# A two-layer decoder trunk on one core: the input turned once, low parts and gate outputs placed differently in layer one, and unread products ahead of the first loads

## The chip, the cores and the metric

The kernel runs on one core of one Trainium2 chip. Its time is the device time of the whole program in microseconds; the number given for a kernel is the median of several runs. TensorE (PE in the profile) multiplies matrices, with a separate queue for loading weights (PEld); VectorE (DVE), ScalarE (ACT) and GpSimd (POOL) do the element work; SyncE (SP) issues nearly all transfers between DRAM and the on-chip memory (SBUF). Products land in PSUM.

## The reference, cut to what matters

Sequence and model width are 1024, one batch, everything in f32. A vector `c` gives shifts, scales and gates for each layer (`ada = silu(c) @ ada_w + ada_b`). Layer one is:

```
h = rmsnorm(x, g0) * (1 + sc1) + sh1
q, k, v, ig, fg, og = split(h @ a_w_in)        # 512, 512, 1024, 8, 8, 1024 columns
hh = mlstm(q, k, v, ig, fg)                    # 8 heads, chunks of 128 tokens, running maximum
y  = (rmsnorm(hh) * sigmoid(og)) @ a_w_out
x  = x + g1 * rmsnorm(y, g1n)
x  = x + g2 * rmsnorm(sqrelu_mlp(rmsnorm(x) * (1 + sc2) + sh2), g3n)
```

Here `rmsnorm(x, g) = x * rsqrt(mean(x*x) + 1e-6) * g`. Layer two (latent attention on shared keys and values, and a second MLP) follows; the change doesn't touch its code.

## The kernel before, in words

**Numbers.** Every large product is made with f32 accuracy out of three matmuls (`mm3`, L235 to L238): each factor is split into a high part, rounded to the fast f32 format (fp32r), and a low part, the difference; the products low x high, high x low and high x high are added in PSUM. Weights come in pieces of 128 x 1024 (`wload`, L209 to L228): SP loads a piece into a tile `raw` (L216), ScalarE casts it to the high part (L193), and the low part is subtracted (L195) by VectorE and GpSimd in turn, by a counter. A variable `low[0]` puts all of them on one engine while it is set; before the change it is set only for the first weights (L1684).

**Layout.** The tokens are handled in two halves of 512, `hfs[0]` and `hfs[1]`. Activations are kept feature-major: eight tiles of 128 features x 512 tokens. The input comes token-major, so it has to be turned by TensorE, four transposes of 128 x 128 for one such tile.

**Buffers.** PSUM is divided among three rotating pools: `ps` (two tiles of 128 x 512), `pc` (two) and `pm` (two double tiles). Four `raw` tiles are shared by the weight pieces and by the pieces of `ada_w` (below).

**Who decides the order.** The program is written as generators that are woven together by hand (`drain`, `weave`, `in_turn`, `with_bg`); a scheduler then orders the instructions of each engine by its own simulated time line. `tc.high_priority` moves an instruction forward and `tc.issue_after` keeps it behind a given one. The order is fixed at build time; on the chip each engine runs its list in order and waits on semaphores.

**Background work.** `ada_chunk` (L353 to L372) computes 512 columns of `ada` on VectorE: four loads of 512 KB, and eight instructions (L363, L365) that multiply 128 rows each by one value of `c` and add, then a few small matmuls (L338 when alone, or four transposes). A version with matmuls (`ada_chunk_pe`, L326) does the shift at the start. `bgs` is a chain of sixteen such chunks, pulled one step at a time by `with_bg` beside other stages.

**The stages around the change**, in program order:

- `vector_columns`, then `first_norm` for half 0: `scale_rows` squares and sums each row on ScalarE (L496), gets 1/rms with some small instructions, multiplies the rows on VectorE (L503), and `turn` transposes them (L524); ScalarE copies the result to SBUF (L1655).
- `ada_first(0)`: the first 512 columns of scale and shift; L1644 makes the factor `A0`.
- The first three weight pieces; `modulate0` for the first four feature tiles (scale and shift on VectorE, L1662; high part on ScalarE, L1663; low part L1665), then `ada_first(1)`.
- `qk_pairs`: queries and keys of half 0, with the other four tiles of `modulate0` in between.
- `gates_in(hfs[0])`, woven with background chunks; it contains `gates0` (L681 to L730), a serial chain of small instructions on 8 x 512 elements, most of them on VectorE.
- `load_x1`; `v_in(hfs[0])` (values) woven with background chunks and `intra0` (the scores within a chunk).
- `scale_x1` (sums of squares and multiplication of the rows of half 1, L505 to L520), and `norm0`: transposes (L530) into `ps`, scale and shift on ScalarE (L532), high part on ScalarE or VectorE (L534), low part on VectorE or GpSimd (L538). `in_turn` weaves it with `og0(hfs[0])` (output gates) and `chunks0(hfs[0])` (the recurrence over chunks).
- For half 1: `gates_in`, `qk_in`, `split_o(hfs[0])` (L784, L786), `v_in` and `intra0`.
- `wout` of half 0 with `chunks0(hfs[1])`; `og0(hfs[1])` woven with `post(hfs[0])`; `wout(hfs[1])` woven with the rest of `post`; then `post(hfs[1])` with the MLP. `post` normalises the output, adds the input (`residual`, L941), and makes the MLP's input (`normed`, L479). The input that it adds comes from `x_rows` (L890): it loads the rows again and turns them again, eight tiles of four transposes (L901) into `pc`.

Of the kernel before, what the change touches and what calls it, by code (L numbers as in the profile page):

```python
# [9 lines left out]
F32 = mybir.dt.float32  # L10
# [4 lines left out]
ALU = mybir.AluOpType  # L15
# [67 lines left out]
def kernel(  # L83
# [69 lines left out]
    def pm():  # L153
        return pp.tile([P, 2, 512], F32, tag="pm", bufs=2, name=f"pm_{next(uid)}")

# [336 lines left out]
    def scale_rows(xt):  # L492
        st = small(4)
        for t in range(4):
            junk = pm()
            nc.scalar.activation(  # L496
                junk.rearrange("p a b -> p (a b)"), xt[t], AF.Square, accum_out=st[:, t : t + 1]
            )
        v, y, w = small(4), small(4), small(4)
        nc.vector.tensor_scalar(v, st, 1.0 / D, EPS, ALU.mult, ALU.add)  # L500
        rsqrt_(y, v, w)
        for t in range(4):
            nc.vector.tensor_scalar(xt[t], xt[t], y[:, t : t + 1], None, ALU.mult)  # L503

    def scale_x1(x1):  # L505
# [7 lines left out]
        v, y, w = small(4), small(4), small(4)  # L513
        nc.vector.tensor_add(v, st[:, 0:4], st[:, 4:8])
        nc.vector.tensor_scalar(v, v, 1.0 / D, EPS, ALU.mult, ALU.add)
        rsqrt_(y, v, w)
# [9 lines left out]
    def norm0(h, xt, A, sh):  # L526
        for k in range(KD):
            pt = ps()
            for t in range(4):
                nc.tensor.transpose(pt[:, ts(t, P)], xt[k // 4][t][:, ts(k % 4, P)], ident)  # L530
            u = tmc()
            nc.scalar.activation(u, pt, AF.Identity, bias=sh[:, k : k + 1], scale=A[:, k : k + 1])  # L532
            if k % 2:
                nc.vector.tensor_copy(h.hi[k], u)  # L534
            else:
                nc.scalar.copy(h.hi[k], u)
            e = nc.vector if k % 2 else nc.gpsimd
            e.tensor_sub(h.lo[k], u, h.hi[k].bitcast(F32))  # L538
# [340 lines left out]
    def wout(w, o, store, wide=False):  # L879

        for m in range(KD):
            pt = proj_fm(w, m * P, o, (lambda: pm()[:, 0]) if wide and m % 2 else ps)
# [6 lines left out]

    def x_rows(half):  # L890

        xt = []
        for t in range(4):
            a = hd() if half else k4()[:, :1024]
            nc.sync.dma_start(a, x_of[half * 4 + t])
            xt.append(a)

        def blk(k):
            pt = pc()
            for t in range(4):  # L900
                nc.tensor.transpose(pt[:, ts(t, P)], xt[t][:, ts(k, P)], ident)  # L901
            return pt

        return blk
# [743 lines left out]
    def first_norm():  # L1648

        scale_rows(x0)  # L1650
# [5 lines left out]
        return xT  # L1656

    def modulate0(h, xT, j):
        A, sh = A0, adac(0, SH1)
        for k in range(4 * j, 4 * j + 4):  # L1660
            u = tmc()
            nc.vector.tensor_scalar(u, xT[k], A[:, k : k + 1], sh[:, k : k + 1], ALU.mult, ALU.add)  # L1662
# [14 lines left out]

    vector_columns()
    xT0 = first_norm()
    drain(ada_first(0, k4))  # L1680

# [27 lines left out]
    def in_turn(wide, steps, fill):  # L1709
# [271 lines left out]
```

## Time and profile before

| what | value |
|---|---|
| median of 3 runs | 2415.41 us (2413.01 to 2417.33) |
| profiled execution, its own time | 2414.08 us |
| its span from first to last instruction | 2412.3 us |
| granted TensorE clock, mean | 0.998 |
| read from and written to DRAM | 313.24 MB and 55.05 MB |
| instructions in the span | 30656 |

The profile is of one execution. It gives the busy time of each engine, divides the span into slices, follows the work that ended last back to the start (the chain of waits), and lists groups of instructions as: line, engine, operation, tile written <- tiles read, shape, count, then busy time and mean length (ns), then the idle time of the engine just before them and what ended it. The timeline lists instructions in order of time as: start, length, engine, line, operation, with the idle time before in brackets. The view of stretches gives busy time per engine in a stretch, then the granted clock (1.00 is full), the share of the 16 DMA engines, and GB/s.

### The profile page before, as it was taken

Reading aid. Unit: us, or ns where it says so; the run is one execution under the profiler, and the core shown is the slowest. Engines: PE = TensorE matmul, PEld = TensorE weight load, DVE = VectorE, ACT = ScalarE, POOL = GpSimd, SP = SyncE. Lnnn points to the kernel's source line nnn. Section 1 sums busy time; section 2 is a strip of 40 time slices with the busy share of each in tenths; the row PEclk is TensorE's granted clock in tenths of the full one; section 3 lists DMA queues with packets and bytes.
Section 4 is the critical chain, followed back from the end, with each engine's and each line's share of the span. In section 5 each row is a group of like instructions: output and inputs, shape, how many; then the busy total and the mean of one; then the engine's idle time right before and its main releaser. Section 6 shows DMA issues by size and latency. Waiting matters only on the chain.

```text
span 2412.3 us, 30656 instructions
## 1 busy us (share of the span) xinstructions
PE 2369.8 (98%) x11669; PEld 1950.5 (81%) x11669; DVE 1476.4 (61%) x2269; ACT 1049.5 (44%) x1706; POOL 435.5 (18%) x269
## 2 busy tenths in 40 slices
PE   7999999999999999999999999999999999999998
PEld 5887787788888887888888877888888888888886
DVE  6576766958665667866664967554555385253335
ACT  4355334645333354434444554434444443443333
POOL 2131221300000000233421100332221102121121
PEclk9999999999999999999999999999999999999999
DMA  7442564444654745555543454774424454354431
GB/s 267 147 130 63 176 191 131 150 133 141 197 175 130 246 133 182 155 168 176 185 131 110 145 161 153 243 250 139 157 97 135 119 162 122 109 188 134 143 103 62
DMA packets 373843, 370.30 MB, mean 154 GB/s; under 512 B 24163, under 2 KB 282272, under 8 KB 373696
## 3 DMA queue, kind: packets, MB, share of 16 engines
q1 hardware_dynamic: 373408, 368.24, 48.6%
q8 instruction: 92, 1.51, 0.3%
q14 instruction: 55, 0.45, 0.1%
q0 software_dynamic: 288, 0.10, 0.0%
HBM read 313.24 MB, written 55.05 MB: 153 GB/s over the span
## 4 chain that ended last, share of the span: by engine, by line
PE 88%; DVE 6%; DMA 3%; ACT 2%; issue 1%; POOL 0%; SPq 0%; DVEq 0%; ACTq 0%
PE ps L236 16%; PE ps L237 16%; PE ps L238 16%; PE pm L236 9%; PE pm L238 9%; PE pm L237 9%; DMA raw<-in_mlp_w_dram 2%; PE pc L1456 1%; PE pc L236 1%; PE pm L811 1%; PE pc L238 1%; PE pc L237 1%; PE pm L1342 1%; PE pm L1336 1%; PE pm L1338 1%
## 5 line engine op out<-in xcount | busy, mean ns | idle before, releaser
L193 ACT CAST wh<-raw 128x1024 fp32r<-128x1024 f32 (+2 forms) x366 | 375.8, 1032 | 740.2 <-PE ps L236 356.3
L195 POOL TENSOR_TENSOR wl<-raw,wh 128x1024 fp32r<-128x1024 f32 (+2 forms) x158 | 379.8, 2409 | 1522.3 <-ACT wh L193 1356.7
L236 PE MATMUL ps<-k,wl 128*128 128x512 f32 x1528 | 611.4, 400 | 6.5 <-DVE wl L195 3.3
L237 PE MATMUL ps<-k,wh 128*128 128x512 f32 x1528 | 601.5, 394 | 0.0
L238 PE MATMUL ps<-k,wh 128*128 128x512 f32 x1528 | 600.8, 393 | 0.0
L195 DVE TENSOR_TENSOR wl<-raw,wh 128x1024 fp32r<-128x1024 f32 (+1 forms) x208 | 270.0, 1301 | 285.1 <-ACT wh L193 278.1
L236 PEld LDWEIGHTS ps<-k,wl 128*128 128x128 f32 x1528 | 287.0, 188 | 74.3 <-DVE wl L195 5.0
L238 PEld LDWEIGHTS ps<-k,wh 128*128 128x128 f32 x1528 | 287.0, 188 | 67.5 <-issue 0.5
L237 PEld LDWEIGHTS ps<-k,wh 128*128 128x128 f32 x1528 | 287.4, 188 | 63.0 <-issue 1.9
L203 DVE TENSOR_TENSOR k<-k,pm 128x512 f32<-128x512 f32 (+1 forms) x254 | 210.7, 859 | 130.3 <-PE pm L238 129.5
L476 DVE TENSOR_TENSOR hd<-tmp,hd 128x512 fp32r<-128x512 f32 x128 | 120.9, 945 | 205.5 <-ACT hd L475 205.2
L236 PE MATMUL pm<-hd,wl 128*128 128x512 f32 x512 | 201.8, 394 | 0.5 <-ACT hd L475 0.5
L237 PE MATMUL pm<-hd,wh 128*128 128x512 f32 x512 | 199.7, 390 | 0.7 <-DVE hd L476 0.7
L238 PE MATMUL pm<-hd,wh 128*128 128x512 f32 x512 | 200.0, 391 | 0.0
L236 PE MATMUL pm<-wh,hd 128*128 128x512 f32 x488 | 192.4, 394 | 2.8 <-ACT raw L1348 2.5
L237 PE MATMUL pm<-wl,hd 128*128 128x512 f32 x488 | 191.3, 392 | 0.0
L238 PE MATMUL pm<-wh,hd 128*128 128x512 f32 x488 | 191.1, 392 | 0.0
L365 DVE SCALAR_TENSOR_TENSOR tma<-raw,cond,tma 128x512 f32<-128x512 f32 x168 | 130.4, 776 | 20.9 <-DMA raw<-in_ada_w_dram 12.1
L1348 ACT ACTIVATE raw<-pm,sm 128x128 f32<-128x128 f32 (+3 forms) x64 | 47.4, 741 | 157.0 <-DVE sm L1347 126.7
L237 PEld LDWEIGHTS pm<-hd,wh 128*128 128x128 f32 x512 | 96.2, 188 | 21.6 <-DVE hd L476 1.0
L236 PEld LDWEIGHTS pm<-hd,wl 128*128 128x128 f32 x512 | 96.1, 188 | 21.4 <-ACT hd L475 0.9
L238 PEld LDWEIGHTS pm<-hd,wh 128*128 128x128 f32 x512 | 96.1, 188 | 21.0
(359 smaller groups left out, 3603.2 us busy)
## 6 DMA issues: line engine op xcount, KB each, us to landing
raw<-in_mlp_w_dram SPq DMA_DIRECT2D x256, 512.0 KB, 4.3
raw<-in_ada_w_dram SPq DMA_DIRECT2D x80, 512.0 KB, 4.4
raw<-in_a_w_in_dram SPq DMA_DIRECT2D x48, 512.0 KB, 4.6
xs<-k SPq DMA_DIRECT2D x40, 256.0 KB, 4.6
raw<-in_kv_ada_w_dram SPq DMA_DIRECT2D x16, 512.0 KB, 4.0
raw<-in_a_w_out_dram SPq DMA_DIRECT2D x16, 512.0 KB, 4.7
kd<-k SPq DMA_DIRECT2D x32, 256.0 KB, 3.5
vd<-k SPq DMA_DIRECT2D x32, 256.0 KB, 5.0
```

What stands on the lines that cost most here:

```text
L193: nc.scalar.copy(hi[:, :n], r[:, :n])
L195: i = e.tensor_sub(lo[:, :n], r[:, :n], hi[:, :n].bitcast(F32))
L203: return f(*a, **k)
L236: nc.tensor.matmul(o, ll, rh, start=start, stop=False)
L237: nc.tensor.matmul(o, lh, rl, start=False, stop=False)
L238: pe_last[0] = nc.tensor.matmul(o, lh, rh, start=False, stop=stop)
L365: nc.vector.scalar_tensor_tensor(acc, r[:, kk], cond[:, k : k + 1], acc, ALU.mult, ALU.add)
L476: nc.vector.tensor_sub(lo, u, hi.bitcast(F32))
L811: nc.tensor.matmul(nv[:, r, i], hf.PT[p_][:, r, cs], v[:, 2 * p_ + r], start=g == 0, stop=True,)
L1336: nc.tensor.matmul(o[:, :w], ql, kh, start=True, stop=False)
L1338: nc.tensor.matmul(o[:, :w], qT, kk[1][:, ks], start=False, stop=False)
L1348: nc.scalar.activation(pr[:, :n], f, AF.Exp, bias=m, scale=SCALE, accum_out=l)
```

## The change

Five parts:

1. **The input is turned once.** `first_norm` and `norm0` turn the raw input instead of rows that were multiplied by 1/rms. The turned tiles are stored to DRAM (`xt_d`): half 0 by four transfers of 512 KB after `qk_pairs`, half 1 by eight of 256 KB within `norm0`. `post` of the first layer loads them from there (`x_ahead(..., True)`), and `x_rows` with its transposes is gone.
2. **1/rms is applied after turning.** `along_tokens` spreads the four columns of 1/rms over a 128 x 512 tile with four matmuls against the identity and a copy by ScalarE. `modulate0` and `norm0` then use one scalar_tensor_tensor on VectorE (input x factor x 1/rms) and the existing `split_mod`: the high part with the shift on ScalarE (L478), the low part by another scalar_tensor_tensor on VectorE (L479). The multiplications of rows and GpSimd's part in them go.
3. **Unread products.** 24 bf16 matmuls of the identity with itself (128 x 512, in a `pc` tile that nothing reads) stand ahead of `vector_columns`, and five more behind the last TensorE instruction of `ada_first(0)`.
4. **Low parts and background.** `low[0]` is VectorE during `v_in`/`intra0` of half 0, and from `gates_in` of half 1 to the end of its `v_in`/`intra0`. `gates_in(hfs[0])` is no longer woven with background chunks. In `in_turn` the filling generator (`norm0`) takes a step every round instead of two of three.
5. **Alternating gates.** In `og0` of half 1 every other product uses a `pm` tile instead of `ps`, as `wout` did already.

```diff
+    def one_pm():
+        return pm()[:, 0]
...
-    def scale_rows(xt):
+    def along_tokens(dst, y):
+        pt = pc()
+        for t in range(4):
+            nc.tensor.matmul(
+                pt[:, ts(t, P)], y[:, t : t + 1].to_broadcast([P, P]), ident, start=True, stop=True
+            )
+        nc.scalar.copy(dst, pt)
+        return dst
+
+    def rms_rows(v):
+        nc.vector.tensor_scalar(v, v, 1.0 / D, EPS, ALU.mult, ALU.add)
+        y, w = small(4), small(4)
+        rsqrt_(y, v, w)
+        return y
+
+    def rms_x0(xt):
...
-        for t in range(4):
-            nc.vector.tensor_scalar(xt[t], xt[t], y[:, t : t + 1], None, ALU.mult)
-
-    def scale_x1(x1):
+        return rms_rows(st)
+
+    def rms_x1(x1):
...
-        for g in range(2):
-            for t in range(4):
-                e = nc.gpsimd if t % 2 else nc.vector
-                e.tensor_scalar(x1[g][t], x1[g][t], y[:, t : t + 1], None, ALU.mult)
+        return rms_rows(v)
...
-    def norm0(h, xt, A, sh):
+    xt_d = [scratch([D, H], f"xt{i}") for i in range(2)]
+
+    def norm0(h, xt, y, A, sh):
+        rstd = along_tokens(tmp(), y)
         for k in range(KD):
             pt = ps()
-            for t in range(4):
-                nc.tensor.transpose(pt[:, ts(t, P)], xt[k // 4][t][:, ts(k % 4, P)], ident)
-            u = tmc()
-            nc.scalar.activation(u, pt, AF.Identity, bias=sh[:, k : k + 1], scale=A[:, k : k + 1])
-            if k % 2:
-                nc.vector.tensor_copy(h.hi[k], u)
-            else:
-                nc.scalar.copy(h.hi[k], u)
-            e = nc.vector if k % 2 else nc.gpsimd
-            e.tensor_sub(h.lo[k], u, h.hi[k].bitcast(F32))
+            turn(xt[k // 4], pt, k % 4)
+            a, u = tmp(), tmc()
+            nc.scalar.copy(a, pt)
+            nc.sync.dma_start(xt_d[1][ts(k, P)], a)
+            nc.vector.scalar_tensor_tensor(u, pt, A[:, k : k + 1], rstd, ALU.mult, ALU.mult)
+            split_mod(h.hi[k], h.lo[k], u, sh[:, k : k + 1])
             yield
...
-            pt = proj_fm(w_in, 2064 + k * P, hf.h)
+            pt = proj_fm(w_in, 2064 + k * P, hf.h, one_pm if hf.i and k % 2 else ps)
...
-    def x_rows(half):
...
-    def x_ahead(alloc):
+    def x_ahead(alloc, first=False):
         def src(half):
             t = [alloc() for _ in range(4)]
+            of = xt_d[half] if first else xs[:, ts(half, H)]
             for b in range(4):
                 nc.sync.dma_start(
-                    t[b], xs[2 * b * P : (2 * b + 2) * P, ts(half, H)].rearrange("(k p) n -> p k n", p=P)
+                    t[b], of[2 * b * P : (2 * b + 2) * P].rearrange("(k p) n -> p k n", p=P)
                 )
...
     def first_norm():
-        scale_rows(x0)
+        y = rms_x0(x0)
...
-        return xT
+        return xT, along_tokens(Cst.rearrange("p a b -> p (a b)")[:, :H], y)
 
     def modulate0(h, xT, j):
...
-            nc.vector.tensor_scalar(u, xT[k], A[:, k : k + 1], sh[:, k : k + 1], ALU.mult, ALU.add)
-            nc.scalar.copy(h.hi[k], u)
-            e = nc.gpsimd if j and k % 2 else nc.vector
-            e.tensor_sub(h.lo[k], u, h.hi[k].bitcast(F32))
+            nc.vector.scalar_tensor_tensor(u, xT[k], A[:, k : k + 1], rs0, ALU.mult, ALU.mult)
+            split_mod(h.hi[k], h.lo[k], u, sh[:, k : k + 1])
...
+    def busy(n):
+        pt = pc()
+        for _ in range(n):
+            i = nc.tensor.matmul(
+                pt, identb, identb.unsqueeze(1).to_broadcast([P, 4, P]), start=True, stop=True
+            )
+        return i.ins.engine
+
+    pe_engine = busy(24)
     vector_columns()
-    xT0 = first_norm()
+    xT0, rs0 = first_norm()
     drain(ada_first(0, k4))
+    with tc.issue_after(last_on_pe()):
+        busy(5)
...
             if n % 3 < 2:
                 go(wide)
-                next(fill, None)
+            next(fill, None)
...
     drain(qk_pairs(hfs[0], w0, modulate0(hfs[0].h, xT0, 1)))
-    drain(with_bg(gates_in(hfs[0]), bgs, 1))
+    for b in range(4):
+        nc.sync.dma_start(
+            xt_d[0][2 * b * P : (2 * b + 2) * P].rearrange("(k p) n -> p k n", p=P), xT0.t[b]
+        )
+    drain(gates_in(hfs[0]))
     x1 = load_x1()
+    low[0] = nc.vector
     drain(weave(with_bg(v_in(hfs[0]), bgs, 1), intra0(hfs[0]), 1.5))
-    scale_x1(x1)
+    low[0] = None
+    y1 = rms_x1(x1)
     hfs[1].h = Split()
-    n1 = norm0(hfs[1].h, x1, A0, adac(0, SH1))
+    n1 = norm0(hfs[1].h, x1, y1, A0, adac(0, SH1))
     in_turn(og0(hfs[0], hdv), chunks0(hfs[0]), n1)
     drain(n1)
 
+    low[0] = nc.vector
     drain(gates_in(hfs[1]))
...
     drain(weave_n(with_bg(main, bgs, 1.7), intra0(hfs[1]), 0.8))
+    low[0] = None
...
-    p0 = post(hfs[0], y0, B0, x_rows, A1, adac(0, SH2))
+    p0 = post(hfs[0], y0, B0, x_ahead(k4v, True), A1, adac(0, SH2))
...
-    p1 = post(hfs[1], y1, B0, x_rows, A1, adac(0, SH2))
+    p1 = post(hfs[1], y1, B0, x_ahead(hdv, True), A1, adac(0, SH2))
```

More of the change, by code (lines that the diff above doesn't have):

```diff
@@ L512, in scale_x1 @@
                 )
[L513 removed]
+        v = small(4)
         nc.vector.tensor_add(v, st[:, 0:4], st[:, 4:8])
[L515 to L520 removed]
+        return rms_rows(v)
     def turn(xt, pt, k):
@@ L881, in wout @@
         for m in range(KD):
-            pt = proj_fm(w, m * P, o, (lambda: pm()[:, 0]) if wide and m % 2 else ps)
+            pt = proj_fm(w, m * P, o, one_pm if wide and m % 2 else ps)
             store(m, pt)
@@ L888 @@
     xs_blk = lambda k, half: xs[ts(k, P), ts(half, H)]
-    def x_rows(half):
[L892 to L904, printed above, removed]
     def x_cols(half):
@@ L1676, in w_parts, with last_on_pe @@
         return [t.rearrange("p (a b) -> p a b", b=256) for t in wsplit(r, D)]
+    def last_on_pe():
+        traced = nc.cur_bb.bb.instructions
+        return next(i for i in reversed(traced) if i.engine == pe_engine)
+    def busy(n):
[6 more added lines that the diff above has]
+    pe_engine = busy(24)
     vector_columns()
-    xT0 = first_norm()
+    xT0, rs0 = first_norm()
     drain(ada_first(0, k4))
+    with tc.issue_after(last_on_pe()):
+        busy(5)
     w0 = [w_raw(b) for b in range(3)]
```

3 lines of the change are left out of this document (removed).

## The prediction

> **What bounds the kernel now.** I read the page first, then the busy time in stretches of 20 us, then the timeline, the chain of waits and the waits of TensorE where a stretch was not full.
>
> ```profile
> span 2412.3 us, 30656 instructions
> PE 2369.8 (98%) x11669; PEld 1950.5 (81%) x11669; DVE 1476.4 (61%) x2269; ACT 1049.5 (44%) x1706; POOL 435.5 (18%) x269
> ```
>
> TensorE is the bound: 42.5 us of the span are without a matmul. So a gain is either TensorE work taken out of full stretches, or idle time. Where the idle time lies (columns: stretch, length, then busy of PE, PEld, DVE, ACT, POOL, then granted clock):
>
> ```profile
> 0.00:20.00 20.00, 6.86 (x26) 4.58 (x26) 12.42 (x38) 9.12 (x17) 6.36 (x21) 1.00 0.91 332
> 20.00:40.00 20.00, 17.80 (x92) 10.61 (x90) 14.45 (x24) 8.68 (x14) 0.00 (x0) 0.91 1.07 367
> 60.00:80.00 20.00, 18.35 (x80) 14.42 (x79) 6.70 (x8) 5.57 (x8) 2.55 (x5) 1.00 0.61 195
> 100.00:120.00 20.00, 18.55 (x147) 16.24 (x145) 14.39 (x29) 9.10 (x25) 2.54 (x1) 1.00 0.25 73
> 120.00:140.00 20.00, 19.58 (x149) 18.50 (x150) 13.81 (x22) 8.53 (x21) 5.16 (x3) 0.91 0.74 223
> 220.00:240.00 20.00, 19.26 (x89) 15.47 (x87) 16.02 (x23) 9.42 (x17) 2.73 (x2) 1.00 0.27 79
> 240.00:260.00 20.00, 18.91 (x110) 14.40 (x108) 18.70 (x29) 6.53 (x13) 6.45 (x2) 1.00 0.18 50
> 260.00:280.00 20.00, 18.07 (x90) 13.97 (x91) 13.10 (x24) 8.66 (x20) 3.71 (x6) 1.00 0.74 216
> ...
> 400.00:420.00 20.00, 20.00 (x91) 16.01 (x90) 11.61 (x14) 13.26 (x23) 3.27 (x2) 1.00 0.62 207
> 420.00:440.00 20.00, 20.00 (x99) 16.45 (x98) 19.18 (x23) 12.51 (x19) 8.01 (x3) 1.00 0.45 140
> ...
> 460.00:480.00 20.00, 19.27 (x84) 15.34 (x83) 19.86 (x21) 13.48 (x20) 12.39 (x11) 1.00 0.15 45
> ```
>
> The start loses 15.3 us (13.1 and 2.2). The first half's stretches lose 1.65 (60 to 80) and 1.87 (100 to 140), where the clock of 0.91 over the second 20 us costs 1.8 more. The second half's gates lose 0.74 + 1.09 + 1.93 = 3.8. The last two rows are the first and the last of three stretches (420 to 480): there TensorE lacks 0.7, but VectorE is as full (19.2 to 19.9 of 20): what is freed there need not arrive. All that the change touches lies before 560 us.
>
> **Part 1: the input turned once.** `x_rows` (L890) turned both halves again ahead of the residual: 2 x 8 blocks x 4 transposes = 64 matmuls of L901.
>
> ```profile
> 427.19 0.87 PE pc L901 x8
> ```
>
> Eight cost 0.87 us on the chain, 0.109 each, so 64 cost 7.0, all in full stretches. Against them stand 8 new transposing products in `along_tokens`; four lie in the idle start, four (0.44) in full stretches: net 6.5. The residual's addition now reads SBUF where it read PSUM, and later stages already do that at the same duration (next fence, L941), so VectorE gains nothing but its waits for L901. The reloads are as large as before (8 x 512 KB). The new stores, 4 x 512 KB from half 0 and 8 x 256 KB from half 1, go on SP's queue. Those of half 0 stand ahead of three weight loads, raw for L590; 2.1 MB at the 367 GB/s of 20 to 40 us is 5.7 us. These loads then come at about 42 to 45 us instead of 37 and are needed from 50, so I count nothing; without that cover it would be up to 3.
>
> ```profile
> L941 DVE TENSOR_TENSOR k<-k,k x16: 682/686/689, 888.7 to 1445.3; 128x512 f32<-128x512 f32 x16
> L941 DVE TENSOR_TENSOR hd<-hd,pc x8: 675/676/689, 430.3 to 448.3; 128x512 f32<-128x512 f32 x8
> ```
>
> Does VectorE let TensorE keep the 6.5? In the rows for 420 and 460 it has 0.8 and 0.1 us free. Its own waits there for L901 go, but the built order puts six more L365 of a background chunk into it. I take 5.5 (bounds 1.5, when VectorE holds the second quarter of the stage, and 6.6).
>
> **Part 2: norms without scaling the rows.** `norm0` on VectorE had 4 casts, 4 subtractions and (in `scale_x1`) 4 multiplications; it gets 16 scalar_tensor_tensor. None reads PSUM at 128x512 here; the nearest are L479 and L365 at 0.75.
>
> ```profile
> L538 DVE TENSOR_TENSOR k<-tmc,k 128x512 fp32r<-128x512 f32 x4 | 2.8, 693 | 0.1
> L534 DVE CAST k<-tmc 128x512 fp32r<-128x512 f32 x4 | 1.7, 426 | 2.0 <-ACT tmc L532 2.0
> L479 DVE SCALAR_TENSOR_TENSOR k<-hd,ada,k 128x512 fp32r<-128x512 f32 x8 | 5.4, 748 | 0.0
> ```
>
> With the multiplications at 0.69 too that is 16 x 0.75 = 12.0 against 2.8 + 1.7 + 2.8 = 7.3: 4.7 us more on VectorE between 140 and 225 us, where it has idle time (16.02 of 20 just after, at 220 to 240) and TensorE sets the pace. Cost 0 (bounds -0.5 and +2, if a `ps` buffer waits for VectorE, since it is now freed by VectorE too and not by ScalarE alone).
>
> **Part 3: the start.** The timeline of the start (start, length, engine, line), and after it two rows of the chain of waits (same columns):
>
> ```profile
> 3.22 0.27 PE L271 MATMUL ps<-ident,tmp 8*128 8x8 f32 x1 [3.22 <-POOL ident masks.py:199]
> ...
> 19.07 1.54 DVE L365 SCALAR_TENSOR_TENSOR tmc<-k,cond,tmc 128x512 f32<-128x512 f32 x2 [0.78 <-DMA k<-in_ada_w_dram]
> ...
> 22.12 1.92 PE L326 MATMUL pc<-k,tma 128*32 128x512 f32 x16
> ...
> 25.27 0.16 DVE L1644 SCALAR_TENSOR_TENSOR mods<-ada,cols 128x4 f32<-128x4 f32 x1
> ...
> 26.64 1.92 DVE L1662 TENSOR_SCALAR tmc<-k,mods,ada 128x512 f32<-128x512 f32 x4
> ...
> 30.62 0.63 PE L236 MATMUL pm<-k,wl 128*128 128x512 f32 x1
> ...
> 31.05 0.63 PE L237 MATMUL pm<-k,wh 128*128 128x512 f32 x1
> ```
>
> ```profile
> 16.53 5.66 PE pc L524 x24
> ...
> 39.05 1.92 PE pc L338 x16
> ```
>
> Now the transposes wait for the norm and hold L326 until 22.12, though its data came about one 512 KB load (1.4 us at 367 GB/s) after the load that VectorE got at 19.07, so at 20.5. After the change the transposes start when x is there (some time before 16.53) and 24 unread products lie before them. These are 128x512, and here such matmuls follow each other by 0.43 at half clock (30.62 to 31.05): 10.3 us at most, from the end of TensorE's first work at 3.5 to 13.8. The 32 transposes, 0.236 each (24 in 5.66), then end at 21.4 at the latest, earlier if the clock rises during the products. I take 20.5: L326's last round of eight ends 1.0 later, at 21.5; L1644 came 1.2 after L326's end and takes 0.16; and the multiplication needs only its scale now, since ScalarE adds the shift. So the first multiplication stands at 22.9 instead of 26.64: 3.7 earlier. But VectorE is then the bound up to L338 at 39.05, and gets more: 4 x (0.75 - 0.48) for the multiplications, 4 x 0.06 for the low parts (a scalar_tensor_tensor at 0.75 for a subtraction at 0.69), and one L195 (1.2 of the 1.30 below) that was done earlier, 2.5 in all. Gain 1.2, bounds 0 (the loads, which run at 367 GB/s, end it) and 3. The gain of a warm clock in the first product block (clock 0.91 in 20 to 40) I count at nothing: it waits for VectorE's low parts in any case.
>
> **Part 4: low parts on VectorE, and gates without background.**
>
> ```profile
> 67.64 1.05 ACT L193 CAST wh<-raw 128x1024 fp32r<-128x1024 f32 x1 [8.42 <-DMA raw<-in_a_w_in_dram]
> ...
> 112.67 2.70 SPq L216 DMA_DIRECT2D raw<-in_a_w_in_dram  x2
> ...
> 117.45 2.91 POOL L195 TENSOR_TENSOR wl<-raw,wh 128x1024 fp32r<-128x1024 f32 x1 [34.83 <-ACT wh L193]
> ```
>
> TensorE's longest wait in 60 to 80, by the waits (us, count, longest):
>
> ```profile
> PE ps L236 <- ACT k L203: 1.6, 1, 1.6
> ```
>
> Both stalls have one root: a weight load that stood on SP behind loads of `ada_chunk`, with which it shares four `raw` buffers. At 60 to 80 ScalarE sat on that load with the evacuation (L203) behind it: 1.65. With `with_bg` gone from the gates, no such load stands ahead of these weights in the built order: gain 1.6 (bounds 0 and 1.7). At 112 the load came late and POOL took 2.91 for the low part, and the clock fell: 1.87 + 1.8 = 3.7. In the new order the third pair of value weights stands ahead of the three chunk loads, and VectorE makes the low part in 1.30 (next fence). The fourth pair still stands behind them. I take 3.0 (bounds 0 and 3.7).
>
> Low parts: 12 move from POOL to VectorE, 12 x 1.30 = 15.6 us of VectorE over 60 to 330 us, each ready 1.1 us sooner than at 2.41.
>
> ```profile
> L195 POOL TENSOR_TENSOR wl<-raw,wh 128x1024 fp32r<-128x1024 f32 (+2 forms) x158 | 379.8, 2409 | 1522.3 <-ACT wh L193 1356.7
> L195 DVE TENSOR_TENSOR wl<-raw,wh 128x1024 fp32r<-128x1024 f32 (+1 forms) x208 | 270.0, 1301 | 285.1 <-ACT wh L193 278.1
> ```
>
> The timeline of VectorE in the two halves' gates, and of TensorE at full clock:
>
> ```profile
> 95.45 0.68 DVE L701 TENSOR_TENSOR tmc<-tmc,tmc 8x512 f32<-8x512 f32 x1
> ...
> 230.07 0.69 DVE L681 COPY tmc<-ps 8x512 f32<-8x512 f32 x1 [2.50 <-PE ps L623]
> ...
> 240.13 2.91 DVE L701 TENSOR_TENSOR tmc<-tmc,tmc 8x512 f32<-8x512 f32 x1
> ...
> 252.61 0.68 DVE L725 TENSOR_TENSOR RM<-tmc,tmc 8x512 fp32r<-8x512 f32 x1
> ```
>
> ```profile
> 36.15 0.39 PE L236 MATMUL pm<-k,wl 128*128 128x512 f32 x1
> ...
> 36.38 0.40 PE L237 MATMUL pm<-k,wh 128*128 128x512 f32 x1
> ```
>
> In the second half's gates they stand in a serial VectorE chain (L681 at 230.1 to L725's end at 253.3: 23.2 us): two L195 (2.6) and two L784 (1.2 each) more within it, 5.0. The built order answers with 119 matmuls, 0.23 apart (27.4 us), between the gate products and the last L730, for a chain of 23.2 + 5.0. So a wait of about 1. Of the 3.8 us I take 1.0 (bounds -2 and 3.5). L701 shows what POOL does to VectorE: 2.91 in the second half, where POOL subtracts beside it, 0.68 in the first, where it doesn't. The Trainium skill (SBUF — State Buffer, "SBUF: two separate sides") says that the two share a port pair which one holds for a whole instruction; the trace agrees with these two durations. By that rule every low part off POOL saves a block of VectorE too, which is rival (c), 2395.6.
>
> **Part 5: alternating gates.** In the second `og0` every other product goes to `pm`. 400 to 420 is full, no wait for a `ps` buffer stands in it: 0. The three background steps moved past the gates come later, on a VectorE that is 58% busy (11.61 of 20) there: 0.
>
> **Sum** against the profiled execution (2414.08, span 2412.3): 5.5 + 1.2 + 1.6 + 3.0 + 1.0 = 12.3, so 2401.8. The median shown is 2415.41, 1.3 above it; I say **2402**.
>
> **Rivals.** (a) *VectorE takes over after 420 us*: 19 to 19.9 of 20 speak for it, the waits for L901 that go speak against; part 1 gives 1.5 and the second half nothing: 2414.1 - 7.3 = 2406.8. (b) *The stalls only move*, since the background loads still share `raw` with the weights: parts 3 and 4 give 0.5 in all, 2414.1 - 6.0 = 2408.1; with (a) too it is 2412. (c) *All stalls go*, with POOL's blocks: 6.6 + 3 + 1.7 + 3.7 + 3.5 = 18.5, 2395.6. (d) *Slower*: the second half's VectorE queue, at 18.70 of 20, becomes the bound between 150 and 330 us; 15.6 + 4.7 = 20.3 us added lie then on the path, 2414.1 - 12.3 + 20.3 = 2422.1. It decides once VectorE has no idle left in these stretches; the rows of these stretches have 1.3 to 7 of 20. That the change doesn't do what it says can be for the products alone (clock still below 1 at 30 us): it would cost nothing here.
>
> **Chances.** Forecast (2398 to 2405) 0.50; (a) or (b) alone 0.23; both 0.06; (c) 0.14; (d) 0.07. The range takes in (a), (b), most of (c): 2394 to 2411. A measurement of this kernel tells about 0.2% (4.8 us) from no change: faster than that 0.85, within 0.08, slower 0.07.
>
> **What would show it.** L901 gone; the multiplications of the first block near 23 and L338 near 38; no wait of TensorE in 60 to 80; clock 1.00 in 120 to 140; TensorE still 20 of 20 from 420 to 480. Idle of TensorE behind L479 or L195 after 420 shows (a), a wait behind `raw` in 100 to 140 shows (b), L730 waiting several us near 250 shows (d). Wrong I would be most if new waits arise that these rows don't show, since the order was built anew up to 560 us.

## The result, and the profile after

The changed kernel takes 2418.72 us (median of 22 runs, 2414.75 to 2424.43), the kernel before 2415.59 (22 runs, 2413.01 to 2418.51): ratio 1.0013, 95% interval 1.0007 to 1.0019. It is 3 us slower, where 13 us faster was forecast; 2418.72 lies above the range of 2394 to 2411. The head of the page of the changed kernel:

```profile
span 2416.2 us, 30620 instructions
PE 2374.9 (98%) x11650; PEld 1949.4 (81%) x11650; DVE 1485.2 (61%) x2283; ACT 1050.9 (43%) x1712; POOL 396.1 (16%) x247
```

The stretches of 20 us of the changed kernel (columns as before: stretch, length, PE, PEld, DVE, ACT, POOL, granted clock, DMA share, GB/s):

```profile
0.00:20.00 20.00, 14.76 (x78) 7.82 (x78) 9.33 (x33) 11.25 (x21) 6.22 (x21) 1.00 0.91 330
20.00:40.00 20.00, 16.62 (x83) 9.94 (x83) 15.75 (x27) 6.77 (x9) 0.00 (x0) 0.91 1.06 382
40.00:60.00 20.00, 20.00 (x82) 16.20 (x82) 10.96 (x16) 8.86 (x13) 6.05 (x7) 0.91 0.64 190
60.00:80.00 20.00, 20.00 (x88) 16.05 (x87) 8.89 (x12) 5.81 (x8) 0.00 (x0) 1.00 0.61 186
100.00:120.00 20.00, 20.00 (x171) 18.63 (x169) 11.94 (x23) 6.35 (x21) 0.00 (x0) 1.00 0.17 53
120.00:140.00 20.00, 20.00 (x163) 18.85 (x163) 15.08 (x26) 11.19 (x29) 2.40 (x1) 1.00 0.69 198
220.00:240.00 20.00, 20.00 (x91) 16.22 (x90) 19.73 (x27) 9.13 (x13) 5.59 (x2) 1.00 0.35 103
240.00:260.00 20.00, 19.55 (x117) 14.60 (x116) 16.61 (x32) 6.47 (x15) 2.58 (x5) 1.00 0.21 57
260.00:280.00 20.00, 19.36 (x119) 15.41 (x115) 13.28 (x21) 6.29 (x13) 0.00 (x0) 1.00 0.74 223
...
420.00:440.00 20.00, 20.00 (x88) 16.22 (x87) 20.00 (x28) 9.67 (x14) 6.62 (x2) 1.00 0.58 175
440.00:460.00 20.00, 14.99 (x52) 10.89 (x51) 17.07 (x19) 11.34 (x19) 7.49 (x2) 0.85 0.74 235
460.00:480.00 20.00, 15.62 (x64) 12.26 (x63) 18.72 (x23) 14.26 (x21) 10.62 (x11) 0.93 0.08 26
480.00:500.00 20.00, 20.00 (x78) 16.07 (x78) 7.91 (x7) 6.00 (x9) 1.93 (x1) 0.88 0.59 158
```

Up to 280 us the forecast holds: the rows from 60 to 140 are full and at full clock, and the second half's gates lose 1.1 where they lost 3.8. How far TensorE is ahead shows in the last copy of the first half's output product out of PSUM, here of the kernel before and then of the changed one (timeline of ScalarE: start, length):

```profile
404.49 0.58 ACT L207 COPY hd<-ps 128x512 f32<-128x512 f32 x1
```

```profile
397.90 0.58 ACT L210 COPY hd<-ps 128x512 f32<-128x512 f32 x1
```

It is 6.6 us ahead, 404.49 - 397.90. Then 440 to 500 takes it back: 5.0 and 4.4 us of idle time, and a clock of 0.85, 0.93 and 0.88, which is 20 x (0.15 + 0.07 + 0.12) = 6.8 more; together 16.2 where the kernel before lost 0.7. Between 660 and 740 us 2.4 more are idle (none before), nearly all of it behind a background chunk (L348 waits for L368). With 7.0 for the transposes that went, 6.6 + 7.0 - 15.5 - 2.4 is about 4 us lost; the two profiled executions differ by 3.9 (2418.01 - 2414.08). What TensorE waited for between 435 and 485 us in the changed kernel (us in total, count, longest):

```profile
PE ps L239 <- POOL wl L198: 4.4, 1, 4.4
PE ps L239 <- ACT k L796: 2.2, 1, 2.2
PE pc L469 <- DVE tmc L465: 1.9, 1, 1.9
PE ps L240 <- POOL k L797: 1.0, 1, 1.0
```

Three of the four are late work of the element engines for the first half's norm (L465) and for the second half's head outputs (L796, L797); the largest is a weight's low part. Two things stand behind them. First, VectorE's queue now holds a whole background chunk (L366, L368: L363, L365 before) just where the residual (L934, L937) is due. The timeline of VectorE, changed kernel:

```profile
415.72 2.51 DVE L366 TENSOR_SCALAR tma<-raw,cond 128x512 f32<-128x512 f32 x1
...
418.82 0.74 DVE L368 SCALAR_TENSOR_TENSOR tma<-raw,cond,tma 128x512 f32<-128x512 f32 x1
...
424.34 5.38 DVE L934 SCALAR_TENSOR_TENSOR hd<-hd,mods,tmc 128x512 f32<-128x512 f32 x8
429.64 0.74 DVE L368 SCALAR_TENSOR_TENSOR tma<-raw,cond,tma 128x512 f32<-128x512 f32 x1
...
438.81 0.73 DVE L368 SCALAR_TENSOR_TENSOR tma<-raw,cond,tma 128x512 f32<-128x512 f32 x1
```

In the kernel before, this chunk was spread over the stretch from 357 to 388 us, where VectorE had time; the first and the last of its six rows there:

```profile
356.62 0.49 DVE L363 TENSOR_SCALAR tma<-raw,cond 128x512 f32<-128x512 f32 x1 [3.56 <-DMA raw<-in_kv_ada_w_dram]
...
386.98 1.54 DVE L365 SCALAR_TENSOR_TENSOR tma<-raw,cond,tma 128x512 f32<-128x512 f32 x2 [1.03 <-DMA raw<-in_kv_ada_w_dram]
```

Second, the place of the first half's norm among the weights of the second half's output product. On ScalarE the high parts of the MLP input (L481; L478 before) stand ahead of the weight casts, and they wait for VectorE's norm (L488). On VectorE the eight low parts of that input (L482; L479 before) run without a gap while GpSimd subtracts the weight's low part. ScalarE, VectorE and GpSimd in the changed kernel:

```profile
465.29 4.70 ACT L481 ACTIVATE k<-hd,ada 128x512 fp32r<-128x512 f32 x7 [3.08 <-DVE hd L488]
470.94 1.05 ACT L196 CAST wh<-raw 128x1024 fp32r<-128x1024 f32 x1 [0.95 <-PE ps L239]
```

```profile
469.82 5.38 DVE L482 SCALAR_TENSOR_TENSOR k<-hd,ada,k 128x512 fp32r<-128x512 f32 x8
```

```profile
472.07 7.08 POOL L198 TENSOR_TENSOR wl<-raw,wh 128x1024 fp32r<-128x1024 f32 x1 [7.09 <-ACT wh L196]
```

The cast stood behind the high parts, but what released it last was TensorE, 0.95 us after they ended. The subtraction took 7.08 us, where this shape takes 2.41 on GpSimd elsewhere (403.82, for one); had it taken 2.41, it would have ended at 474.5, just before TensorE ran dry (474.8). So the 4.4 us are GpSimd's delay beside VectorE.

The order is the same in the kernel before, and GpSimd's subtraction was as slow. There it cost 0.7 us, since TensorE came to it later and still had products to do:

```profile
463.15 5.36 ACT L478 ACTIVATE k<-hd,ada 128x512 fp32r<-128x512 f32 x8 [3.88 <-DVE hd L485]
468.42 1.03 ACT L193 CAST wh<-raw 128x1024 fp32r<-128x1024 f32 x1
```

```profile
469.53 7.51 POOL L195 TENSOR_TENSOR wl<-raw,wh 128x1024 fp32r<-128x1024 f32 x1 [7.48 <-ACT wh L193]
```

### The profile page after: what moved, and what is told of

The parts are those of the page before. It is cut to its first block, busy times and chain, and to the rows that moved or that the text cites. A ratio compares the mean times of both kernels' runs of the same rounds, so it can differ in the third digit from the quotient of the medians.

```text
span 2416.2 us, 30620 instructions
## 1 busy us (share of the span) xinstructions
PE 2374.9 (98%) x11650; PEld 1949.4 (81%) x11650; DVE 1485.2 (61%) x2283; ACT 1050.9 (43%) x1712; POOL 396.1 (16%) x247
## 4 chain that ended last, share of the span: by engine, by line
PE 82%; DVE 7%; DMA 7%; ACT 2%; issue 1%; SPq 0%; POOL 0%; DVEq 0%; ACTq 0%
PE ps L239 15%; PE ps L240 15%; PE ps L241 15%; PE pm L239 9%; PE pm L240 9%; PE pm L241 9%; DMA raw<-in_mlp_w_dram 4%; PE pc L1452 1%; ACT wh L196 1%; DVE wl L198 1%; DVE tma L368 1%; PE pc L239 1%; PE pc L240 1%; PE pc L241 1%; PE pm L1338 1%
## 5 line engine op out<-in xcount | busy, mean ns | idle before, releaser
L239 PE MATMUL ps<-k,wl 128*128 128x512 f32 x1496 | 601.1, 402 | 6.6 <-POOL wl L198 4.4
L198 POOL TENSOR_TENSOR wl<-raw,wh 128x1024 fp32r<-128x1024 f32 (+2 forms) x146 | 355.2, 2438 | 1508.5 <-ACT wh L196 1183.9
L241 PE MATMUL ps<-k,wh 128*128 128x512 f32 x1496 | 590.4, 395 | 0.0
L240 PE MATMUL ps<-k,wh 128*128 128x512 f32 x1496 | 589.0, 394 | 1.0 <-POOL k L797 1.0
L198 DVE TENSOR_TENSOR wl<-raw,wh 128x1024 fp32r<-128x1024 f32 (+1 forms) x220 | 280.5, 1278 | 298.8 <-ACT wh L196 293.6
L241 PEld LDWEIGHTS ps<-k,wh 128*128 128x128 f32 x1496 | 281.9, 188 | 66.8 <-issue 0.2
L240 PEld LDWEIGHTS ps<-k,wh 128*128 128x128 f32 x1496 | 282.6, 189 | 63.8 <-POOL k L797 1.4
L479 DVE TENSOR_TENSOR hd<-tmp,hd 128x512 fp32r<-128x512 f32 x128 | 120.6, 942 | 204.6 <-ACT hd L478 204.3
L368 DVE SCALAR_TENSOR_TENSOR tma<-raw,cond,tma 128x512 f32<-128x512 f32 x168 | 127.6, 759 | 9.6 <-DMA raw<-in_ada_w_dram 7.8
L240 PEld LDWEIGHTS pm<-hd,wh 128*128 128x128 f32 x512 | 96.2, 188 | 21.7 <-DVE hd L479 1.0
L964 ACT ACTIVATE tmp<-ps 128x512 f32<-128x512 f32 x128 | 75.8, 592 | 87.0 <-PE ps L241 86.9
```

The source lines that it names most:

```text
L198: i = e.tensor_sub(lo[:, :n], r[:, :n], hi[:, :n].bitcast(F32))
L239: nc.tensor.matmul(o, ll, rh, start=start, stop=False)
L240: nc.tensor.matmul(o, lh, rl, start=False, stop=False)
L241: pe_last[0] = nc.tensor.matmul(o, lh, rh, start=False, stop=stop)
L368: nc.vector.scalar_tensor_tensor(acc, r[:, kk], cond[:, k : k + 1], acc, ALU.mult, ALU.add)
L479: nc.vector.tensor_sub(lo, u, hi.bitcast(F32))
```

## The experiments

The theories: **C**, the chunk on VectorE; **Q**, ScalarE's queue, in which the high parts hold the weight casts; rivals **P** (the second turning paced the additions), **G** (GpSimd's low part beside VectorE is the cause by itself) and **S** (VectorE's chain starts too late, since its sum is pulled behind the third gate product). Each run was compared with the kernel before on its own chip, whose median there was 2414.3 to 2416.2; where two runs are set against each other, the difference is of their medians, and the one by these ratios (times 2415.6) follows in brackets where it differs. The 95% interval of such a difference reaches 3 to 4 us to each side.

**e1_bg_back**, the changed kernel with background beside the gates again:

```diff
-    drain(gates_in(hfs[0]))
+    drain(with_bg(gates_in(hfs[0]), bgs, 1))
```

> The changed kernel with the background chunk pulled beside the first half's gates again (three steps earlier from there on). Theory C (a whole chunk, eight VectorE instructions and 8.3 us, was moved from 357 to 387 us into 415 to 439 us, where VectorE sets the pace): its instructions stand at 357 to 388 again, TensorE's idle time between 440 and 480 falls from 9.4 us to under 3, the 1.6 us stall at 60 to 80 comes back, and the time falls from 2418.7 to about 2410. Theory P (without the transposes of the input, the eight additions of the input stand in one block ahead of the head products of the second half, and so the last output product comes late): the block stays, so the idle time stays above 7 us and the time is 2417 to 2421. Theory G (GpSimd's subtractions and the 2.5 to 8.7 us that VectorE's instructions take beside them): likewise 2417 to 2421.

Measured: 2412.25, ratio 0.9994 (0.9986 to 1.0003). 6.5 less than the changed kernel (4.6): the way C said, against P and G as the only cause, but half to three quarters of what C said (2410). The wait at 460 to 480 stayed (6.5 us), where C had put all idle time of 440 to 480 under 3.

**e2_bg_in_wout**, the gates free, three steps of the chain taken later:

```diff
-        wout(a_w_out[0], hfs[0].o, ...), chunks0(hfs[1]), iter(())
+        wout(a_w_out[0], hfs[0].o, ...), chunks0(hfs[1]), (next(bgs) for _ in range(3))
```

> The changed kernel, gates of the first half still without background, but three steps of the background chain are taken in the output product of the first half, so that the chunks stand as before from there on. Theory C: idle time of 440 to 480 under 3 us and no stall at 60 to 80, so about 1.6 below the run with the background beside the gates: 2408. Theories P and G: 2417 to 2421.

Measured: 2408.38, ratio 0.9973 (0.9962 to 0.9985), 10.3 less than the changed kernel (9.7), as C said. The three smaller waits of 440 to 460 are gone. But the idle time is not under 3, since one wait is left, the only one between 400 and 500 us:

```profile
PE ps L239 <- POOL wl L198: 6.5, 1, 6.5
```

ScalarE in this run shows what stands ahead of it: the eight high parts, and then, without a gap, the cast. GpSimd's subtraction behind it is slow again:

```profile
459.77 5.37 ACT L481 ACTIVATE k<-hd,ada 128x512 fp32r<-128x512 f32 x8 [3.87 <-DVE hd L488]
465.04 1.04 ACT L196 CAST wh<-raw 128x1024 fp32r<-128x1024 f32 x1
```

```profile
466.15 7.46 POOL L198 TENSOR_TENSOR wl<-raw,wh 128x1024 fp32r<-128x1024 f32 x1 [7.48 <-ACT wh L196]
```

TensorE ran dry at 467.2. With a subtraction of 2.41 the low part would have been there at 468.6, so by estimate 5 of the 6.5 us are GpSimd's and 1.4 the late cast's.

**e3_before_gates_free**, that one line of the change alone, in the kernel before:

```diff
-    drain(with_bg(gates_in(hfs[0]), bgs, 1))
+    drain(gates_in(hfs[0]))
```

> The kernel before with only one part of the change: the gates of the first half without background. Theory C: the stall at 60 to 80 (1.6) goes, the chunk falls into 415 to 439, and the time rises by 5 to 9 to 2420 to 2424. Theory P: no block of additions here, since the transposes pace them: 2413 to 2415. Theory G: no GpSimd work was added: 2413 to 2415.

Measured: 2427.79, ratio 1.0054 (1.0040 to 1.0067): 13 slower, more than C's 5 to 9. The stall of 60 to 80 is gone, the chunk lies at 424 to 444, and the stretch behind it is

```profile
440.00:460.00 20.00, 16.62 (x70) 12.77 (x69) 18.41 (x23) 12.79 (x20) 6.97 (x3) 0.83 0.76 238
```

which lacks 3.4 of TensorE, all of it in transposes (L901) that wait for VectorE's additions (L941), and 3.4 of clock. The rest lies elsewhere (2.5 of idle time in 280 to 400, 2.3 in 600 to 800, none there before), with the other chunks that the three steps moved.

**e4_turned_again**, the changed kernel with `x_rows` and its 64 transposes back:

```diff
-    p0 = post(hfs[0], y0, B0, x_ahead(k4v, True), A1, adac(0, SH2))
+    p0 = post(hfs[0], y0, B0, x_rows, A1, adac(0, SH2))
...
-    p1 = post(hfs[1], y1, B0, x_ahead(hdv, True), A1, adac(0, SH2))
+    p1 = post(hfs[1], y1, B0, x_rows, A1, adac(0, SH2))
```

> The changed kernel with the input turned a second time for the residual, as before (the stores of the turned input stay, but are not read). Theory C: the chunk stays in 415 to 439; the 64 transposes (7 us) come back, half of them into TensorE's idle time: 2420 to 2424. Theory P: the additions are paced again and the idle time of 440 to 480 goes: 2418.7 - 9.4 + 7 = 2416 or less. Theory G: 2420 to 2425.

Measured: 2408.99, ratio 0.9979 (0.9970 to 0.9988). With 7 us more for TensorE it is 9.7 faster (8.2), against C as put and as P said. The pace of the additions is not the only thing that differs, though: in this built order ScalarE's casts and copies for the output product stand ahead of and between the high parts, and GpSimd's subtractions take 2.59 and 2.69. That is where Q comes from.

**e5_bg_and_early_sum** and **e6_early_sum** pull the sum of squares one gate product earlier, on e2 and on the changed kernel:

```diff
         if k < 7:
             next(p0)
+        if k == 1:
+            next(p0)
```

> The changed kernel with the three background steps in the output product (as two runs above) and the first half's sum of squares over the features taken one gate product earlier. Theory S (the stretch of 415 to 475 us is bound by VectorE's chain from that sum to the MLP's input; its start is fixed by program order behind the third gate product, so what TensorE gained before is waited for): the sum moves from 414.8 to about 409, the chain ends 5 to 6 us earlier, the wait of 6.5 us at 467 and most of the clock loss of 3.4 us go: about 2400. Theory G (that wait is GpSimd's low part, 7.4 us beside VectorE instead of 2.4): the wait stays, 2407 to 2409.

> The changed kernel with only that sum taken one gate product earlier; the background chunk stays in 415 to 439. Theory S: 4 to 7 us less, 2412 to 2415, with the chunk still in the way. Theory C alone (only the chunk matters): within 2 us of 2418.7.

Measured: 2404.46, ratio 0.9964 (0.9951 to 0.9976), and 2410.21, ratio 0.9983 (0.9974 to 0.9992): 3.9 less than e2 (2.2, within the noise), 8.5 less than the changed kernel (7.2). The chain started 7 us earlier in both, and in the changed kernel its start counts. But a wait of 4.5 us stayed in e5, again for GpSimd, whose subtraction L797 took 8.38 us there: S is a part at most, not the cause.

**e7_bg_and_turned_again** joins e2 and e4.

> The changed kernel with the three background steps in the output product and the input turned a second time. Transposes 7 us back. If TensorE's work in the bound stretch is free (theory S: it waits there anyway, 6.5 us and 3.4 of clock): 2406 to 2410, the same as without the transposes. If taking the transposes away was worth what they cost (7 us): 2415.

Measured: 2403.95, ratio 0.9959 (0.9946 to 0.9971), below both numbers: 4.4 less than e2 (3.4, about the noise) though 64 transposes came back. TensorE has no idle time from 400 to 800.

**e8_no_products** and **e12_no_products** take the 29 unread products out, of the changed kernel and of e7.

> The changed kernel without its 29 unread products. Theory S says that nothing gained before 415 us arrives, so the time is within 2 us of 2418.7 whatever the products do to the start. By the prediction's own count they are free (0). A rival: they delay the first transposes or cost clock, then the first product block starts earlier without them and the trace shows it between 20 and 46 us.

> The same kernel of 2403.95 us without the 29 unread products, where what the start gains can arrive. The prediction counted the products as free and without gain: within 1 us of 2404. Rival: the products' warm clock matters, 1 to 2 us more without them. Second rival: they cost, since 7.1 us of products stand ahead of the first transposes: 1 us less.

Measured: 2417.10, ratio 1.0009 (1.0000 to 1.0017), against 1.0013 with them; and 2404.81, ratio 0.9949 (0.9936 to 0.9962), against 0.9959. Both differences lie within the intervals and point to no effect.

**e9_casts_ahead** takes e2, pulls the first five pieces of the second half's output product ahead, and keeps the norm behind the cast of the fifth weight, on ScalarE and all other engines alike:

```diff
+    w1 = wout(a_w_out[0], hfs[1].o, store1, True)
+    for _ in range(5):
+        next(w1)
+    third = cast[0]
+    def behind(g):
+        while True:
+            with tc.issue_after(third):
+                v = next(g, StopIteration)
...
-    drain(weave(wout(a_w_out[0], hfs[1].o, store1, True), p0, 1.25))
+    drain(weave(w1, behind(p0), 1.25))
```

> The changed kernel with the three background steps in the output product, and the normalisation that makes the first half's MLP input kept behind the cast of the fifth weight of the second half's output product. Theory Q (on ScalarE, eight high parts of the MLP input stand ahead of the weight casts and wait there for VectorE, so TensorE runs out of weights at 467 us; with the second turning the scheduler interleaves them, and that is why the transposes looked useful): the wait of 6.5 us and the clock loss of 3.4 us go, 2408.4 - 8 = 2399 to 2402. Theory S (VectorE's chain itself is late): the wait only moves behind the MLP's first product, 2406 to 2409.

Measured: 2399.98, ratio 0.9932 (0.9919 to 0.9944): 8.4 less than e2 (9.9), Q's number, and the fastest of all. But the edit does two things: ScalarE's cast now waits for TensorE and comes 3.7 us earlier than in e2, and VectorE's norm is held back too, so that GpSimd's low part takes 2.41 and not 7.46. This run does not tell the two apart; e13 below does. Timelines of ScalarE and GpSimd (lines are one higher in this kernel):

```profile
461.31 1.05 ACT L197 CAST wh<-raw 128x1024 fp32r<-128x1024 f32 x1 [5.58 <-PE ps L240]
...
468.88 0.72 ACT L482 ACTIVATE k<-hd,ada 128x512 fp32r<-128x512 f32 x1 [2.11 <-DVE hd L489]
```

```profile
462.44 2.41 POOL L199 TENSOR_TENSOR wl<-raw,wh 128x1024 fp32r<-128x1024 f32 x1 [4.06 <-ACT wh L197]
```

Two of its stretches, from the 60 us in which the changed kernel lost 16:

```profile
440.00:460.00 20.00, 20.00 (x86) 15.89 (x86) 17.36 (x21) 9.17 (x15) 5.46 (x7) 1.00 0.51 146
460.00:480.00 20.00, 20.00 (x88) 16.26 (x87) 16.17 (x19) 16.55 (x26) 4.96 (x6) 1.00 0.44 126
```

**e10_casts_ahead_early** adds the early sum to e9.

> As the run just named, and the first half's sum of squares one gate product earlier. Theory Q and S together: 2396 to 2400, and TensorE full from 400 to 600 us. If Q alone holds, the same as the run just named; if S alone, 2401 to 2404.

Measured: 2406.17, ratio 0.9955 (0.9942 to 0.9968): 6 slower than e9 (5.6), so neither theory's number. TensorE now waits 2.0 us at 443 for the data of the sum itself, which stands earlier in its queue. Of the rest, 2.5 lie at the start of the profiled execution (0.7 of TensorE, and a clock of 0.74 over 20 to 40 where e9 had 0.83), where the edit does nothing, and 0.5 in 340 to 360. With the norm behind the cast, an earlier start of the chain brings nothing.

**e11_low_alternating** puts the low parts of e7 back to GpSimd and VectorE in turn:

```diff
-    low[0] = nc.vector
     drain(weave(with_bg(v_in(hfs[0]), bgs, 1), intra0(hfs[0]), 1.5))
...
-    low[0] = nc.vector
     drain(gates_in(hfs[1]))
```

> The kernel of 2403.95 us (background steps in the output product, input turned twice) with the weights' low parts of the first layer alternating between GpSimd and VectorE as before. By the prediction the low parts are worth part of 3.0 us at 100 to 140 and 1.0 in the second half's gates: 2 to 4 us more, 2406 to 2408, with a stall near 112 to 118 and VectorE instructions of 2.6 to 2.9 us in the second half's gates. Rival (only the loads' order mattered): within 1 us of 2404.

Measured: 2416.75, ratio 1.0004 (0.9995 to 1.0013): 12.8 slower than e7 (by the ratios 0.0045 x 2415 = 11), where 2 to 4 was expected. TensorE lacks 3.1 in 220 to 280 (1.0 in e7), 2.1 in 280 to 400 (0.5) and 2.9 in 600 to 800 (0).

**e16_before_low_vector** is the counterpart, those low parts on VectorE alone, in the kernel before.

> The kernel before with one part of the change: the low parts of the first half's values and of the second half's layer one on VectorE. From the run with alternating low parts (12.8 us lost on the kernel of 2404): up to 10 us gained where it can arrive. From the changed kernel's lesson (VectorE and ScalarE between 415 and 475 don't get earlier by it): the gain at 100 to 140 and 220 to 280 comes to about 5, and the wait at 465 to 475 takes most of it back, 2412 to 2415. A gain of 8 or more, 2407 or less, speaks against the lesson.

Measured: 2419.03, ratio 1.0021 (1.0010 to 1.0033): 4.5 slower, outside both numbers. 100 to 140 gains 1.3 and the clock's 1.8, but 140 to 220 loses 1.9, and 220 to 280 lacks 4.3 (3.8 before) with a clock of 0.83 in its last 20 us (1.00 before; 3.4 us). So the low parts are worth 11 on e7 and less than nothing on the kernel before. Which part of the rest decides that was not tried and stays open.

**e13_after_casts_ahead** and **e14_before_casts_ahead** make the edit of e9 in the changed kernel and in the kernel before.

> The changed kernel, background as changed (the chunk stays in 415 to 439), with only the norm kept behind the cast of the fifth weight. Theory Q (ScalarE's queue makes the loss): the 4.4 us wait and part of the clock loss at 460 to 500 go, the waits of 5 us at 447 to 455 (head outputs, sum) stay: 2409 to 2412. Theory C first (the chunk is what makes VectorE late): less than 4 us gained, 2415 to 2418.

> The kernel before with only the norm kept behind that cast. ScalarE's queue is in the same order there, but TensorE comes to it 6 to 8 us later and waits 0.7 us. Theory Q: 0 to 1.5 us gained, 2413.5 to 2415.5. Against it: 4 us or more, as if the order were bad in itself.

Measured: 2410.43, ratio 0.9985 (0.9977 to 0.9994), 8.3 less than the changed kernel (6.8), in the range put for Q; and 2412.50, ratio 0.9992 (0.9984 to 1.0001), 2.0 less than the kernel before, a little over Q's 1.5 and at the edge of the noise. This order is nearly free where TensorE comes late to it, and costs 7 to 8 where it comes early. In e13 the waits of TensorE between 400 and 500 us are just the three that e2 had removed:

```profile
PE ps L240 <- ACT k L797: 2.2, 1, 2.2
PE pc L470 <- DVE tmc L466: 1.9, 1, 1.9
PE ps L241 <- POOL k L798: 1.0, 1, 1.0
```

And the cast comes no earlier than in the changed kernel (470.94 there), since it waits for TensorE in both. What is new is the subtraction:

```profile
471.57 1.05 ACT L197 CAST wh<-raw 128x1024 fp32r<-128x1024 f32 x1 [8.86 <-PE ps L240]
```

```profile
472.69 2.41 POOL L199 TENSOR_TENSOR wl<-raw,wh 128x1024 fp32r<-128x1024 f32 x1 [7.35 <-ACT wh L197]
```

So Q has the right place and the wrong engine here: the wait of 4.4 us went because VectorE's norm no longer runs beside GpSimd's subtraction, not because ScalarE's queue got free. No run moved that one low part to VectorE, which would show it by itself. The two causes add up within the noise: 10.3 (e2) + 8.3 (e13) = 18.6 (16.5), and both together (e9) give 2418.72 - 2399.98 = 18.7 (19.6).

**e15_casts_ahead_turned_again** turns the input twice in e9.

> The kernel of 2399.98 us (background steps in the output product, norm behind the cast) with the input turned a second time. With the queue free in both, the 64 transposes are worth what the prediction counted: 6.5 net, so 2405 to 2407. Rival (the transposes lie in waiting time anyway): 2400 to 2402.

Measured: 2404.27, ratio 0.9963 (0.9951 to 0.9976): 4.3 more than e9 by the medians, 7.5 by the ratios. With the norm behind the cast the transposes only cost, about the 6.5 that was counted; that their pace helps (P) is not seen here.

## Why the prediction was wrong

The failing step is the last sentence of part 5: the three background steps "come later, on a VectorE that is 58% busy there: 0". They shift the whole chain of chunks, and one chunk of eight instructions (2.51 + 7 x 0.74 = 7.7 us) came into 415 to 439, not into 400 to 420; the prediction's own row for 420 to 440 had VectorE at 19.18 of 20. The cost was about 10 (e2), and the one line alone makes the kernel before 13 slower (e3). Part 1 had noted "six more L365" in that stage from the built order (seven came, and one L363) and charged 1.0 for them.

The second is that terms of different stages were added although a fixed point lies between them. The gains of parts 3 and 4 were there, 6.6 us at 405; but between 415 and 475 the norm on VectorE, with GpSimd's subtraction held up beside it, keeps its own time, and TensorE, coming earlier, waited. Rival (a) named the place, and its sign came (TensorE idle behind L198, which is L195 before), but it was priced too low: it took 5.0 from the sum, part 1's gain and the second half's, and left the earlier gains in it. And waiting cost more than was gained, since the two long waits brought 6.8 us of clock with them.

By the steps (in the sum, 2402 leaves out the 1.3 by which the median lies above the profiled execution; 2403 would follow, which changes nothing):

- Part 1: the transposes are worth 4 to 7.5 (e15 against e9; counted 5.5, bounds 1.5 to 6.6), but only with the norm behind the weight casts. In the changed kernel they were worth -8 to -10 (e4): with them TensorE has none of the waits of 440 to 480, and GpSimd's subtraction takes 2.59 and not the 7.08 that it takes beside the block of low parts in the order built without them. How much each of these is worth there stays open. The bound of 1.5 from below was the error.
- Part 2: nothing. Right: TensorE has 79.9 of 80 us in 140 to 220.
- Part 3: the first multiplication was put at 22.9; it starts at 23.16. But the gain of 1.2 did not stay. The small matmuls of `ada_first(1)` (L341; L338 before) start at 37.64 (39.05 before; counted near 38), and then a second stretch at low clock, 0.91 over 40 to 60, costs 1.8. Before, that stretch was at 1.00; but e3, e14 and e16, which have the start of the kernel before, lose 3.4 to 3.6 of clock between 20 and 60 as the changed kernel does, so this loss is not shown to come from the change.
- Part 4: the stall of 60 to 80 went (1.65; counted 1.6), that of 100 to 140 with its clock (3.7; counted 3.0), and the gates lost 1.1 for 3.8 (2.7; counted 1.0). Right in kind, 2.4 too low (8.0 for 5.6). The price of its low parts by themselves was not understood (e11, e16).
- Part 5: alternating gates, no wait seen, not tried alone; the background steps, above.

The rows that should have warned were in the trace of before: L478 eight times from 463.15, L193 at 468.42, and then 7.51 us for a GpSimd subtraction that takes 2.41 elsewhere, with VectorE at 19.86 of 20. Whoever asks of these rows "what if TensorE is here 6 us earlier" finds the wait of 6.5 us that e2 shows. e9, with both causes removed, measures 2399.98 where the forecast was 2402. That is in part luck: by its ratio e9 gains 16.4 where 12.3 was counted, part 4 was 2.4 too low, the start's gain did not stay, and e9's own edit gains about 2 in the kernel before too (e14).

## What to carry to other kernels

Between the place where time is gained and the end, look for the first stretch where another engine is full and in order, and ask which instructions there, on it or on an engine that it slows, TensorE's next work waits for: a gain ahead of that point is worth only the slack it has. Where background work is pulled by steps, dropping steps in one place moves every later chunk, so list where each comes to lie. A part that does less work can still cost, when the order built without it is another one: compare the queues of all engines, and what runs beside what, not only counts.

## What was not expected of the hardware

A GpSimd subtraction of 128x1024 takes 2.4 us, and beside a VectorE that runs without a gap far more: 7.08 us in the changed kernel, 7.51 in the kernel before and 7.46 in e2, each beside eight low parts of VectorE in a row (5.4 us). In e9 and e13, with the norm held back, it took 2.41. The profile counts the time as busy time of GpSimd, so no wait of GpSimd shows it.

The prediction had looked only at what GpSimd does to VectorE (2.91 for 0.68); it goes the other way too. The Trainium skill (SBUF — State Buffer, "SBUF: two separate sides") describes the shared pair of ports as held by one of the two for a whole instruction; these durations agree. That a row of short instructions on one side can keep the other waiting for the whole row is what they add. It doesn't always: in e4 the subtractions at 463.60 and 467.64 took 2.59 and 2.69 beside eight L488, and VectorE lost instead, 9.70 us for the eight where e2 has 5.39. What decides that stays open.

The clock also fell with the long gaps. In the changed kernel the granted clock was 0.50 from 456 to 460 us, behind three waits of 5.0 us in all, and 0.50 again from 478 to 484, behind the wait of 4.4; the matmuls there (128x512) stand 0.43 us apart and not 0.23. So here 9.4 us of idle time brought 6.8 of clock. In e4, e7, e9 and e15 TensorE has no gap in 400 to 500 us, and the clock is 1.00. Shorter gaps did it in some places only: after 1.9 us idle in 680 to 700 of the changed kernel the clock stayed at 1.00, with 2.0 us idle there in e6 it was 0.91.
